# Gated delta rule in a 1-core fp32 network: the inverse of the 32x32 diagonal triangles by matmul levels, or by substitution on VectorE

## The chip, the cores and the metric

The kernel runs on one core of one Trainium2 chip. Its time is the device time of one launch in microseconds (us); of several runs the median counts. PE is TensorE, PEld its weight loads, DVE is VectorE, ACT is ScalarE, POOL is GpSimd, SP is the queue that issues the DMAs of this kernel. One row of the trace is one instruction; an f32 matmul shows as two rows, a matmul with fp32r operands as one.

## The reference, cut to what matters

The network is a mixer block with an MLP, then a gated delta-rule layer with 8 heads, a convolutional FFN, a sliding-window attention layer and a second FFN, on 512 positions of 1024 features. The change is in the delta-rule layer. With `q, k, v` of a head (512 x 128 each), `beta` and a decay `g` per position:

```python
decay = exp(where(i >= j, gc[i] - gc[j], -inf))      # gc: running sum of g inside a chunk
Lmat  = where(i > j, (k * beta) @ k.T * decay, 0)
sol   = triangular_solve(eye + Lmat, [v * beta, k * beta * exp(gc)])
# then, chunk by chunk:
v_new = value - k_cumdecay @ state
o     = q_dec @ state + attn_intra @ v_new
state = state * exp(gc_last) + k_dec.T @ v_new
```

The reference uses chunks of 64 positions; both kernels use 4 blocks of 128, which gives the same numbers in another grouping. Each head needs the inverse of four lower triangular 128x128 matrices with ones on the diagonal.

## The kernel before, in words

All activations are kept transposed (features on the 128 partitions, 512 positions along a row). A dense layer multiplies in three passes, hi*hi, hi*lo and lo*hi of a split into two fp32r parts (`mm3`, L269 to L273); a unit is one output tile of 128 features: 8 steps of `mm3`, 24 matmuls of 512 columns, into one of three PSUM buffers tagged `mm` (tile `m` in the trace). Five more PSUM buffers, tagged `aux` (tile `a`), serve all else. `weights` (L238) loads 512 KB by SP, rounds it on ACT (L247) and subtracts on DVE (L248); three buffers of each kind let it run three loads ahead.

The delta layer has 24 units for k, q, v of 8 heads, each followed by a causal convolution (`conv4`: L609, L610, three times L612, L614), and 8 gate units. `delta_begin` does the first 5 units, the scalars of all heads, and the decay matrices E of all 8 heads (`decay`: two matmuls L730 and L731 and four Exp on ACT, L734). `delta` then writes the rest out by hand with `weave`, which draws from several generators in proportion to the step counts given with them. While 23 steps of dense units are drawn, each of four stages moves on for one head each:

- `delta_a`: transposes of k, q, v, the norms (squares on ACT, L754 and L758, a Newton root on POOL), the matrix LT (L776), the matrix AT (L794), and kd, vb (L780, L781).
- `delta_b`: the inverse T of the four 32x32 diagonal triangles of each block by four levels, each of two rounds of four matmuls of 128x128 by 32 columns (`mmc`, L650), with masks on DVE (L807, L809), a DVE transpose (L643) and copies that spread the result on the diagonal (`expand`, L637, L639).
- `delta_b2`: merges 32 into 64 and 64 into 128 (L830, and `mm4` L657 on halves), then one correction step in f32 with two full rounds (L854, L860).
- `delta_c`: the recurrence over the four blocks (L875 to L899), the output norm (L903 to L911) and the transposes of the output.

Then `gated` (L974) multiplies by the gate and splits, and `OutProj` does the output layer; its first three tiles can start as heads become ready (`head`), the other five after all (`rest`). The order that each engine runs is not quite the order of the code: the framework takes the instructions by priority, which follows the code, but passes over those that it does not reckon ready, so a later dense matmul may stand before an earlier small one. At run time each engine keeps that fixed order.

Of the kernel before, what the change touches and what calls it, by code (L numbers as in the profile page):

```python
# [10 lines left out]
F32 = mybir.dt.float32  # L11
F32R = mybir.dt.float32r
# [53 lines left out]
SD = 6, 6, 13  # L66
FILL = 23
TAIL = (1.2, 1.3, 2.0, 3.0)
# [3 lines left out]
def _pack(i):  # L72
# [55 lines left out]
    for n in range(2):  # L128
# [14 lines left out]
    lev = [(((i[:, None] // (2 * s)) == (i[None, :] // (2 * s))) & ((i[:, None] // s) % 2 == 1)  # L143
            & ((i[None, :] // s) % 2 == 0)) for s in (1, 2, 4, 8, 16)]
    lev = [-t.astype(np.float32) for t in [lev[0].T] + lev[1:]] + [np.eye(P, dtype=np.float32)]
    a["levels"] = np.ascontiguousarray(np.concatenate(
        [np.concatenate([t[q:q + Q, q:q + Q] for q in range(0, P, Q)]) for t in lev], axis=1))
# [38 lines left out]
class Net:  # L186
    def __init__(self, ctx, tc, a, out, stages):
# [8 lines left out]
        self.sp = e(tc.tile_pool(name="sp", bufs=12))  # L196
        self.n = 0
# [435 lines left out]
    def expand(self, out, src):  # L633
        for i, q in enumerate(self.quads()):
            o, t = self.v4(out)[q, :, q], self.c4(src)[q]
            if i % 2:
                self.nc.scalar.copy(out=o, in_=t)  # L637
            else:
                self.nc.vector.tensor_copy(out=o, in_=t)  # L639

    def flip(self, src):
        t = self.sized(P, "cm", 6)
        self.nc.vector.transpose(out=t, in_=src.bitcast(F32))  # L643
        return t

    def mmc(self, lhs, rhs):
        ps = self.aux()
        for b in range(NB):
            c = slice(b * Q, (b + 1) * Q)
            self.nc.tensor.matmul(ps[:, c], lhsT=self.blk(lhs, b), rhs=rhs[:, c], start=True, stop=True)  # L650
        return self.c4(ps)

# [14 lines left out]
    def delta_scalars(self, ps, y):  # L667
# [47 lines left out]
        rows = self.hid(F32R)[0:ROWS]  # L715
        A.copy(out=rows, in_=pr[0:ROWS])
        lo = slice(Q, ROWS)
        V.tensor_tensor(out=rows[lo], in0=pr[lo], in1=rows[lo].bitcast(F32), op=ALU.subtract)
        sel = [self.hid(F32R)[0:ROWS] for _ in range(2)]
        for i, t in enumerate(sel):  # L720
            one = self.ident[0:ROWS, 4 * i:4 * i + 4].unsqueeze(2).to_broadcast([ROWS, 4, P])
            V.tensor_copy(out=self.v4(t), in_=one)
            V.tensor_copy(out=self.v4(t)[lo], in_=one[0:8])
# [23 lines left out]
    def delta_a(self, h):  # L747
        nc, d, s = self.nc, self.d, self.heads[h]
        V, A = nc.vector, nc.scalar
        E = self.E[h]  # L750
# [12 lines left out]
        sc = self.sized(20, "hs", 4)  # L763
        x, z, inv, rkl, rem = (sc[:, i * NB:(i + 1) * NB] for i in range(5))
        rk = r[:, 0:4]
        for o, t, u in ((x, rk, d["beta"][:, :, h]), (z, x, rk), (inv, v[:, 0:4], rk), (rkl, rk, d["ekl"][:, :, h]),
                        (rem, z, ss[:, 0:4])):
            nc.gpsimd.tensor_tensor(out=o, in0=t, in1=u, op=ALU.mult)
        nc.gpsimd.tensor_scalar(out=rem, in0=rem, scalar1=-1.0, scalar2=1.0, op0=ALU.mult, op1=ALU.add)
# [12 lines left out]
        yield  # L782
        LTr = self.hid(F32R)
        A.copy(out=LTr, in_=LT)
        LD, TD = (t[h % 2] for t in self.diag[:2])
        C, T = self.sized(P, "cm", 6), self.sized(P, "Tc", 3, F32R)
        for q in self.quads():
            A.copy(out=self.v4(LD)[q, :, q], in_=self.v4(LT)[q, :, q])
            V.tensor_tensor(out=self.c4(C)[q], in0=self.v4(LT)[q, :, q], in1=self.rep(self.lev[0], q), op=ALU.mult)
        V.tensor_tensor(out=self.c4(C), in0=self.c4(C), in1=self.rep(self.lev[5]), op=ALU.add)  # L790
# [6 lines left out]
        self.expand(TD, C)  # L797
        A.copy(out=T, in_=self.flip(C))
        self.heads[h] = dict(LT=LT, LTr=LTr, AT=AT, T=T, k=s["k"], kd=kd, vb=vb, q=s["q"], x=x, rem=rem, rq=r[:, 4:8])

    def delta_b(self, h):
        nc, d, s = self.nc, self.d, self.heads[h]
        V, A = nc.vector, nc.scalar
        T, (LD, TD, TL, TTL) = s["T"], (t[h % 2] for t in self.diag)
        for l in range(1, 5):
            M = self.sized(P, "cm", 6, F32R)
            V.tensor_tensor(out=self.c4(M), in0=self.mmc(LD, T), in1=self.rep(self.lev[l]), op=ALU.mult)  # L807
            yield
            V.tensor_tensor(out=self.c4(T), in0=self.mmc(TD, M), in1=self.c4(T).bitcast(F32), op=ALU.add)  # L809
            self.expand(TTL if l == 4 else TD, self.flip(T))  # L810
            yield
        self.expand(TL, T.bitcast(F32))

    def delta_b2(self, h):
        nc, d, s = self.nc, self.d, self.heads[h]
        V, A = nc.vector, nc.scalar
        LT, LTr = s["LT"], s["LTr"]
        T, TT = (t[h % 2] for t in self.diag[2:])
        T4, TT4, L4 = self.v4(T), self.v4(TT), self.v4(LTr)
        M = self.sized(P, "cm", 6, F32R)  # L820
        m4 = self.c4(M)
        pairs = [(slice(c, c + Q), slice(c + Q, c + 2 * Q)) for c in (0, 64)]

        def small(lo, hi, *fs):
            ps = self.aux()
            o = [self.c4(ps[:, i * P:]) for i in range(len(fs))]
            for t, f in zip(o, fs):
                for b in range(NB):
                    lhs, rhs = f(lo, hi, b)
                    nc.tensor.matmul(t[0:Q, b], lhsT=lhs, rhs=rhs, start=True, stop=True)  # L830
            return [t[0:Q] for t in o]

        for lo, hi in pairs:
            p, = small(lo, hi, lambda lo, hi, b: (L4[lo, b, hi], T4[lo, b, lo]))
            A.mul(m4[hi], p, -1.0)
        yield
        for lo, hi in pairs:
            p2, p3 = small(lo, hi, lambda lo, hi, b: (TT4[hi, b, hi], m4[hi, b]),
                           lambda lo, hi, b: (m4[hi, b], TT4[hi, b, hi]))
            A.copy(out=T4[hi, :, lo], in_=p2)  # L840
            V.tensor_copy(out=TT4[lo, :, hi], in_=p3)
        yield
        M = self.tmp(F32R)
        m4 = self.v4(M)
        top, bot = slice(0, 64), slice(64, P)
        p1 = self.mm4(LTr, T, k=top, m=bot, n=top)
        A.mul(m4[bot, :, top], self.v4(p1)[top, :, top], -1.0)
        yield
        p2, p3 = self.mm4(TT, M, k=bot, m=bot, n=top), self.mm4(M, TT, k=bot, m=top, n=bot)
        A.copy(out=T4[bot, :, top], in_=self.v4(p2)[top, :, top])  # L850
        V.tensor_copy(out=TT4[top, :, bot], in_=self.v4(p3)[top, :, bot])
        yield
        G = self.hid()
# [11 lines left out]
    def delta_c(self, h):  # L865
# [4 lines left out]
        for n in range(NB):  # L870
# [13 lines left out]
            if n < NB - 1:  # L884
                nc.tensor.matmul(p[:, 3 * P:], lhsT=B("kd"), rhs=vn, start=True, stop=True)  # L885
# [395 lines left out]
```

## Time and profile before

| | us |
|---|---|
| median of 3 runs | 1933.41 |
| the 3 runs | 1938.40, 1921.08, 1933.41 |
| span of the profiled execution, first to last instruction | 1936.9 |
| PE busy in it | 1901.8 (98%) |
| DVE busy | 1255.4 (65%) |
| ACT busy | 854.1 (44%) |
| mean granted clock of TensorE | 0.986 |

The span is that of one execution; the page gives no separate time for what lies around it, and the span lies inside the range of the three runs. The delta layer's decay block starts at 672.5 us of the span, its woven part ends about 977, and its last output tile about 1024. Busy time of PE counts overlapped rows once.

### The profile page before, as it was taken

To read this page: it belongs to the slowest core of one execution; us is meant where nothing else is said; L and a number is where in the kernel's file an instruction comes from. 1 tells how busy PE (TensorE), PEld (TensorE's weight loads), DVE (VectorE), ACT (ScalarE), POOL (GpSimd) and SP (SyncE) were. 2 spreads that over 40 slices of the span, in tenths; PEclk is the share of its full clock that TensorE was granted. 3 is DMA by queue.
4 is the path that set the end of the run, shared out by engine and by line. 5 is a ranking of instruction groups with operands and counts; after the bars stand their busy time and mean duration, and the time that the engine had idled before them with its cause. 6 is when DMAs were issued, how large, how long until landed. Compare 5 with 4: busy or idle time off the path is not lost.

```text
span 1936.9 us, 24978 instructions
## 1 busy us (share of the span) xinstructions
PE 1901.8 (98%) x9566; PEld 1587.6 (82%) x9566; DVE 1255.4 (65%) x2405; ACT 854.1 (44%) x1621; POOL 47.0 (2%) x162
## 2 busy tenths in 40 slices
PE   8999999999999999999999999999999999999997
PEld 6887888888889778888877888888889878888887
DVE  7999677324535847887776777743566567777434
ACT  5324443222333576675544444432367644444221
POOL 0010000000000011201000000000000000000000
PEclk9999999999999988998999999999999999999999
DMA  4222222222222211111122223222221122222221
GB/s 174 98 93 98 93 82 89 98 98 98 98 98 87 70 65 44 36 53 34 44 83 92 98 97 95 94 96 98 98 71 44 56 87 98 98 98 98 98 98 55
DMA packets 48520, 164.84 MB, mean 85 GB/s; under 512 B 5776, under 2 KB 8592, under 8 KB 48400
## 3 DMA queue, kind: packets, MB, share of 16 engines
q1 hardware_dynamic: 48400, 163.25, 24.4%
q8 instruction: 75, 1.23, 0.3%
q14 instruction: 45, 0.37, 0.1%
HBM read 161.13 MB, written 2.10 MB: 84 GB/s over the span
## 4 chain that ended last, share of the span: by engine, by line
PE 90%; DVE 5%; ACT 2%; issue 1%; POOL 0%; DMA 0%; SPq 0%; DVEq 0%; ACTq 0%
PE m L271 27%; PE m L272 27%; PE m L273 27%; PE a L657 1%; PE a L1207 1%; PE a L650 1%; PE a L623 1%; DVE t L612 1%; PE a L1146 1%; PE a L1188 1%; DVE wl L248 1%; ACT wh L247 1%; PE a L349 0%; PE a L880 0%; PE a L885 0%
## 5 line engine op out<-in xcount | busy, mean ns | idle before, releaser
L271 PE MATMUL m<-xh,wh 128*128 128x512 f32 (+1 forms) x1560 | 606.9, 392 | 10.9 <-ACT xh L305 7.0
L272 PE MATMUL m<-xl,wh 128*128 128x512 f32 (+1 forms) x1560 | 605.3, 389 | 0.5
L273 PE MATMUL m<-xh,wl 128*128 128x512 f32 (+1 forms) x1560 | 603.6, 388 | 0.5 <-DVE wl L248 0.5
L247 ACT CAST wh<-wr 128x1024 fp32r<-128x1024 f32 x302 | 316.6, 1051 | 604.3 <-PE m L272 473.4
L248 DVE TENSOR_TENSOR wl<-wr,wh 128x1024 fp32r<-128x1024 f32 x302 | 368.3, 1221 | 249.0 <-ACT wh L247 245.3
L271 PE MATMUL m<-h,wh 128*128 128x512 f32 (+1 forms) x984 | 362.7, 370 | 2.5 <-DVE x L1045 0.9
L273 PE MATMUL m<-h,wl 128*128 128x512 f32 (+1 forms) x984 | 362.9, 369 | 0.0
L272 PE MATMUL m<-h,wh 128*128 128x512 f32 (+1 forms) x984 | 362.8, 369 | 0.0
L271 PEld LDWEIGHTS m<-xh,wh 128*128 128x128 f32 x1560 | 294.2, 190 | 69.3 <-ACT xh L305 7.6
L273 PEld LDWEIGHTS m<-xh,wl 128*128 128x128 f32 x1560 | 296.0, 190 | 58.3 <-DVE wl L248 1.2
L272 PEld LDWEIGHTS m<-xl,wh 128*128 128x128 f32 x1560 | 295.8, 190 | 56.3 <-DVE xl L306 2.4
L271 PEld LDWEIGHTS m<-h,wh 128*128 128x128 f32 x984 | 185.3, 189 | 35.6 <-issue 2.0
L273 PEld LDWEIGHTS m<-h,wl 128*128 128x128 f32 x984 | 185.6, 189 | 31.7 <-DVE wl L248 0.9
L272 PEld LDWEIGHTS m<-h,wh 128*128 128x128 f32 x984 | 185.6, 189 | 31.5 <-issue 0.7
L1022 DVE SCALAR_TENSOR_TENSOR t<-t,vecs,t 128x511 f32<-128x511 f32 (+1 forms) x176 | 131.5, 747 | 4.9 <-ACT t L1020 1.8
L1019 DVE TENSOR_TENSOR t<-m,R 128x512 f32<-128x512 f32 x88 | 60.5, 687 | 83.3 <-PE m L273 83.3
L302 ACT CAST h<-t 128x512 fp32r<-128x512 f32 x80 | 49.6, 622 | 145.3 <-DVE t L1030 120.9
L497 DVE SCALAR_TENSOR_TENSOR h<-h,vecs,h 128x511 f32<-128x511 f32 (+28 forms) x120 | 82.3, 727 | 0.9 <-ACT h L494 0.9
L303 DVE TENSOR_TENSOR h<-t,h 128x512 fp32r<-128x512 f32 x80 | 55.1, 689 | 29.7 <-ACT h L302 29.5
L1020 ACT ACTIVATE t<-t,vecs 128x512 f32<-128x512 f32 x88 | 71.6, 814 | 1.7 <-DVE t L1019 1.6
L1028 ACT ACTIVATE t<-t 128x512 f32<-128x512 f32 x44 | 27.8, 632 | 85.2 <-DVE t L1022 85.2
L579 DVE TENSOR_TENSOR t<-m,R 128x512 f32<-128x512 f32 x32 | 22.1, 689 | 58.6 <-PE m L273 56.7
(268 smaller groups left out, 1688.6 us busy)
## 6 DMA issues: line engine op xcount, KB each, us to landing
wr<-in_f_up SPq DMA_DIRECT2D x88, 512.0 KB, 3.5
wr<-in_f_down SPq DMA_DIRECT2D x44, 512.0 KB, 3.4
wr<-in_w_up SPq DMA_DIRECT2D x32, 512.0 KB, 3.4
wr<-in_w_down SPq DMA_DIRECT2D x32, 512.0 KB, 3.4
wr<-in_a_w_in SPq DMA_DIRECT2D x32, 512.0 KB, 3.5
wr<-in_w_in SPq DMA_DIRECT2D x28, 512.0 KB, 3.5
wr<-in_w_o SPq DMA_DIRECT2D x8, 512.0 KB, 3.5
wr<-in_a_w_out SPq DMA_DIRECT2D x8, 512.0 KB, 3.5
```

Source lines behind the costliest of these rows:

```text
L247: nc.scalar.copy(out=wh, in_=raw)
L248: nc.vector.tensor_tensor(out=wl, in0=raw, in1=wh.bitcast(F32), op=ALU.subtract)
L271: nc.tensor.matmul(ps, lhsT=w[0], rhs=x[0], start=start, stop=False)
L272: nc.tensor.matmul(ps, lhsT=w[0], rhs=x[1], start=False, stop=False)
L273: nc.tensor.matmul(ps, lhsT=w[1], rhs=x[0], start=False, stop=stop)
L302: nc.scalar.copy(out=hi, in_=src)
L303: nc.vector.tensor_tensor(out=lo, in0=src, in1=hi.bitcast(F32), op=ALU.subtract)
L497: nc.vector.scalar_tensor_tensor(out=c[:, d:], in0=v[:, :S - d], scalar=wt[CONV_K - 1 - d], in1=c[:, d:], op0=ALU.mult, op1=ALU.add)
L1019: V.tensor_tensor(out=u, in0=ps, in1=R, op=ALU.mult)
L1020: A.activation(out=y, in_=u, func=AF.Identity, scale=w[2], bias=self.vec(f"f_b{i}", c))
L1022: V.scalar_tensor_tensor(out=y[:, d:], in0=u[:, :S - d], scalar=w[2 - d], in1=y[:, d:], op0=ALU.mult, op1=ALU.add)
L1028: A.activation(out=g, in_=g, func=AF.Silu)
```

## The change: what it does, and its diff

E is computed head by head inside `delta_a` instead of in `delta_begin`. LT gets the opposite sign. `delta_a` no longer makes the rounded copy and the compact copy of the diagonal; instead it writes the four 32x32 diagonal pieces of each block to a scratch in HBM (4 DMAs a head, runs of 128 bytes). `delta_solve` reads the 64 triangles of 4 heads back as 64 partitions of 1024 elements, does the forward substitution with 60 `tensor_tensor` on DVE, writes the inverse out and gathers it with one DMA as 128 partitions by 16 runs of 128 bytes. `delta_merge` merges 32 to 64 to 128 for 4 heads at once, in f32. The correction step is gone. `delta_c` writes `vn` over `vb` and the state over `kd`. The weave runs in two groups of 4 heads.

```diff
-SD = 6, 6, 13
-FILL = 23
-TAIL = (1.2, 1.3, 2.0, 3.0)
+SD = 6, 11, 14
+GROUP = 4
...
+        self.dp = e(tc.tile_pool(name="dp", bufs=4, space=bass.MemoryType.DRAM))
...
     def delta_a(self, h):
...
-        E = self.E[h]
+        E = self.decay(h)
...
+        nc.gpsimd.tensor_scalar(out=z, in0=z, scalar1=-1.0, scalar2=None, op0=ALU.mult)
...
+        L4, scr = self.v4(LT), self.scr[h // GROUP][0]
+        for i, q in enumerate(self.quads()):
+            nc.sync.dma_start(out=scr[h % GROUP, :, i].rearrange("b j i -> j b i"), in_=L4[q, :, q])
         kd, vb = self.hid(), self.hid()
...
-        LTr = self.hid(F32R)
-        A.copy(out=LTr, in_=LT)
...
-    def delta_b(self, h):
...
-    def delta_b2(self, h):
...
+    def delta_solve(self, g):
+        nc = self.nc
+        V = nc.vector
+        src, dst = self.scr[g]
+        W = self.sized(Q * Q, "solve", 1)[0:GROUP * 4 * NB]
+        nc.sync.dma_start(out=W, in_=src.rearrange("h b d j i -> (h b d) (j i)"))
+        S3 = W.rearrange("p (j i) -> p j i", i=Q)
+        n = GROUP * 4 * NB
+        yield
+        for j in range(1, Q - 1):
+            w = Q - 1 - j
+            t = self.sized(240, "outer", 2)[0:n, :j * w].rearrange("p (c i) -> p c i", i=w)
+            V.tensor_tensor(out=t, in0=S3[:, j:j + 1, j + 1:].to_broadcast([n, j, w]),
+                            in1=S3[:, 0:j, j:j + 1].to_broadcast([n, j, w]), op=ALU.mult)
+            V.tensor_tensor(out=S3[:, 0:j, j + 1:], in0=S3[:, 0:j, j + 1:], in1=t, op=ALU.add)
+            yield
+        V.memset(W[:, ::Q + 1], 1.0)
+        nc.sync.dma_start(out=dst.rearrange("h b d j i -> (h b d) (j i)"), in_=W)
+        TT = self.hid()
+        nc.sync.dma_start(out=TT.rearrange("p (h b i) -> p h b i", h=GROUP, b=NB),
+                          in_=dst.rearrange("h b d j i -> (d j) h b i"))
+        self.inv[g] = TT
+        yield
+
+    def delta_merge(self, g):
...
+        V.transpose(out=Tc, in_=TTc)
...
+        for k in (0, 2):
+            lo, hi = q[k], q[k + 1]
+            p = self.aux()
+            for i in range(n):
+                s, b = at(i)
+                T.matmul(p[0:Q, i * Q:(i + 1) * Q], lhsT=self.v4(s["LT"])[lo, b, hi], rhs=Tq[lo, i], start=True, stop=True)
+            (A.copy if k else V.tensor_copy)(out=M[hi], in_=p[0:Q])
             yield
+        for i, s in enumerate(hs):
+            for d in range(4):
+                o, t = s["t4"][q[d], :, q[d]], TTq[q[d], i * NB:(i + 1) * NB]
...
+        for i in range(n):
+            T.matmul(p[0:Q, i * Q:(i + 1) * Q], lhsT=TTq[q[1], i], rhs=Mq[q[1], i], start=True, stop=True)
+        A.copy(out=T64[q[1], :, 0:Q], in_=cq(p)[0:Q])
+        yield
+        for k in (0, 2):
+            p = self.aux()
+            for i in range(n):
+                T.matmul(p[0:Q, i * Q:(i + 1) * Q], lhsT=Mq[q[k + 1], i], rhs=TTq[q[k + 1], i], start=True, stop=True)
...
+        for h in range(0, GROUP, 2):
+            p, M = self.aux(), self.hid()
+            p4, M4 = (t.rearrange("p (n c) -> p n c", c=64) for t in (p, M))
+            for i in range(2 * NB):
+                s, b = at(h * NB + i)
+                T.matmul(p4[top, i], lhsT=self.v4(s["LT"])[top, b, bot], rhs=T64[top, h * NB + i], start=True, stop=True)
+            A.copy(out=M[bot], in_=p[top])
+            yield
+            p = self.aux()
...
+            for i in range(2 * NB):
+                s, b = at(h * NB + i)
+                T.matmul(p4[top, i], lhsT=M4[bot, i], rhs=s["t4"][bot, b, bot], start=True, stop=True)
...
-        self.E = [self.decay(h) for h in range(HEADS)]
...
     def delta(self):
...
-        for i in range(1, HEADS):
-            self.weave((islice(fill, FILL), FILL),
-                       *((f(i - 1 - j), n) for j, (f, n) in enumerate(stages) if i > j))
...
+        units = lambda n: (islice(fill, n * NT), n * NT)
+        a, c = self.delta_a, self.delta_c
+        self.weave(units(4), (chain(a(0), a(1)), 2 * SD[0]))
+        self.weave(units(3), (a(2), SD[0]))
+        self.weave(units(3), (a(3), SD[0]))
+        self.weave(units(6), (self.delta_solve(0), 36))
+        self.weave(units(1), (self.delta_merge(0), SD[1]))
+        self.weave(units(1), *((c(h), SD[2]) for h in range(4)))
+        self.weave(units(2), (chain(a(4), a(5)), 2 * SD[0]), (a(6), 2 * SD[0]))
+        self.weave(units(1), (a(7), SD[0]))
+        self.weave(units(5), (self.delta_solve(1), 36))
+        for h in range(4):
+            gated(h)
+        self.weave(units(1), (self.delta_merge(1), SD[1]))
 
         def rest():
             yield from fill
...
             yield from out.head(4)
...
+        self.weave((rest(), NT + 12), *((c(h), SD[2]) for h in range(4, 8)))
+        for h in range(4, 8):
+            gated(h)
         out.rest()
```

## Rows read from the trace of the kernel before

**Rows 1.** The page, part 1: busy time of each engine over the span
```profile
PE 1901.8 (98%) x9566; PEld 1587.6 (82%) x9566; DVE 1255.4 (65%) x2405; ACT 854.1 (44%) x1621; POOL 47.0 (2%) x162
```

**Rows 2.** Windows: us, then busy us (x instructions) per engine, clock, DMA
```profile
672.50:693.00 20.50, 20.27 (x43) 11.50 (x44) 5.29 (x8) 11.49 (x36) 0.00 (x0) 0.58 0.14 51
693.00:977.00 284.00, 275.79 (x1779) 233.69 (x1777) 220.19 (x698) 184.79 (x593) 37.40 (x144) 0.95 0.14 47
...
1030.00:1390.00 360.00, 359.08 (x1582) 296.47 (x1581) 223.52 (x279) 145.90 (x179) 0.00 (x0) 1.00 0.28 96
```

**Rows 3.** Timeline of PE in the decay block: start, us, instruction
```profile
673.13 0.50 PE L731 MATMUL a<-h,identr 128*128 128x512 f32 x1
673.57 0.50 PE L730 MATMUL a<-h,h 40*128 40x512 f32 x1
...
674.33 0.40 PE L271 MATMUL m<-xh,wh 128*128 128x512 f32 x1
```

**Rows 4.** Groups of PE by line in the delta layer (640 to 1030)
```profile
L731 PE MATMUL a<-h,identr 128*128 128x512 f32 x8 | 5.8, 720 | 0.0
```

**Rows 5.** Timeline of PE in the woven stretch, small matmuls in pieces
```profile
935.89 0.42 PE L657 MATMUL a<-t,h 64*64 64x64 f32 x4
936.14 0.40 PE L657 MATMUL a<-h,t 64*64 64x64 f32 x4
936.47 0.49 PE L880 MATMUL a<-h,h 128*128 128x128 f32 x2
936.71 0.47 PE L271 MATMUL m<-xh,wh 128*128 128x512 f32 x1
...
937.49 0.51 PE L650 MATMUL a<-Tc,h 128*128 128x32 f32 x4
937.85 0.66 PE L623 MATMUL a<-c,h 128*128 128x128 f32 x4
938.27 0.47 PE L271 MATMUL m<-xh,wh 128*128 128x512 f32 x1
...
939.49 1.06 PE L657 MATMUL a<-h,h 128*128 128x128 f32 x8
940.30 0.47 PE L271 MATMUL m<-xh,wh 128*128 128x512 f32 x1
...
944.38 0.31 PE L830 MATMUL a<-h,h 32*32 32x32 f32 x8
944.61 0.50 PE L271 MATMUL m<-xh,wh 128*128 128x512 f32 x1
```

**Rows 6.** Groups of DVE by line in the delta layer
```profile
L248 DVE TENSOR_TENSOR wl<-wr,wh 128x1024 fp32r<-128x1024 f32 x41 | 49.8, 1219 | 2.1 <-ACT wh L247 1.9
L612 DVE SCALAR_TENSOR_TENSOR t<-t,vecs,t 128x511 f32<-128x511 f32 (+2 forms) x57 | 41.9, 738 | 1.9 <-ACT t L610 1.5
...
L609 DVE TENSOR_TENSOR t<-m,R 128x512 f32<-128x512 f32 x19 | 13.0, 682 | 17.6 <-ACT h L614 15.5 <-PE m L273 2.0
...
L807 DVE TENSOR_TENSOR cm<-a,h 128x128 fp32r<-128x128 f32 x32 | 9.1, 286 | 8.7 <-PE a L650 8.4
```

**Rows 7.** Groups of ACT by line in the delta layer
```profile
L780 ACT ACTIVATE h<-a,hs 128x128 f32<-128x128 f32 x32 | 12.2, 382 | 0.4 <-POOL hs L768 0.3
...
L758 ACT ACTIVATE t<-a 128x128 f32<-128x128 f32 x32 | 8.5, 276 | 0.9 <-PE a L623 0.7
...
L758 ACT ACTIVATION_READ_ACCUMULATOR t<-a 128x1 f32 x32 | 6.6, 207 | 0.1
...
L614 ACT ACT_TABLE_LOAD x1 | 1.3, 1283 | 0.0
```

**Rows 8.** DMA queues, and issues with KB each and us to landing
```profile
q1 hardware_dynamic: 48400, 163.25, 24.4%
...
wr<-in_a_w_in SPq DMA_DIRECT2D x32, 512.0 KB, 3.5
```

**Rows 9.** Waits of the SP queue, 640 to 1000: us, times, longest
```profile
SPq L246 <- DVE wl L248: 231.1, 24, 27.5
```

More of the change, by code (lines that the diff above doesn't have):

```diff
@@ L631, in quads @@
             yield slice(q, q + Q)
[L633 to L651, printed above, removed]
     def mm4(self, lhs, rhs, k=slice(0, P), m=slice(0, P), n=slice(0, P)):
@@ L714, in delta_scalars @@
             nc.tensor.transpose(self.blk(pr, b)[0:ROWS], gx[:, b, :], self.ident)
-        rows = self.hid(F32R)[0:ROWS]
-        A.copy(out=rows, in_=pr[0:ROWS])
+        rows = self.hid(F32R)
+        nc.gpsimd.memset(rows.bitcast(F32), 0.0)
+        A.copy(out=rows[0:ROWS], in_=pr[0:ROWS])
         lo = slice(Q, ROWS)
         V.tensor_tensor(out=rows[lo], in0=pr[lo], in1=rows[lo].bitcast(F32), op=ALU.subtract)
-        sel = [self.hid(F32R)[0:ROWS] for _ in range(2)]
+        sel = [self.hid(F32R) for _ in range(2)]
         for i, t in enumerate(sel):
-            one = self.ident[0:ROWS, 4 * i:4 * i + 4].unsqueeze(2).to_broadcast([ROWS, 4, P])
+            one = self.ident[:, 4 * i:4 * i + 4].unsqueeze(2).to_broadcast([P, 4, P])
             V.tensor_copy(out=self.v4(t), in_=one)
@@ L781, in delta_a @@
             A.activation(out=self.blk(vb, b), in_=self.blk(pv, b), func=AF.Copy, scale=inv[:, b:b + 1])
-        yield
-        LTr = self.hid(F32R)
-        A.copy(out=LTr, in_=LT)
[L785 to L790, printed above, removed]
         yield
@@ L814, in delta_b2 @@
-    def delta_b2(self, h):
[L815 to L835, printed above, removed]
-        yield
[L837 to L853, printed above, removed]
-        p = self.mm4(LT, T.bitcast(F32))
-        for b in range(NB):
-            V.scalar_tensor_tensor(out=self.blk(G, b), in0=self.blk(T, b).bitcast(F32),
-                                   scalar=s["rem"][:, b:b + 1], in1=self.blk(p, b), op0=ALU.mult, op1=ALU.add)
-        yield
-        U = self.hid()
-        V.scalar_tensor_tensor(out=U, in0=TT.bitcast(F32), scalar=2.0, in1=self.mm4(G, TT.bitcast(F32)),
-                               op0=ALU.mult, op1=ALU.subtract)
-        yield
-        s["TT"] = U
@@ L880, in delta_c @@
             nc.tensor.matmul(p[:, 0:P], lhsT=B("TT"), rhs=w, start=True, stop=True)
-            vn = self.sized(P, "vn", 3)
-            A.activation(out=vn, in_=p[:, 0:P], func=AF.Copy, scale=s["x"][:, n:n + 1])
+            A.activation(out=w, in_=p[:, 0:P], func=AF.Copy, scale=s["x"][:, n:n + 1])
             yield
+            new = B("kd")
             if n < NB - 1:
-                nc.tensor.matmul(p[:, 3 * P:], lhsT=B("kd"), rhs=vn, start=True, stop=True)
-            nc.tensor.matmul(p[:, 2 * P:3 * P], lhsT=B("AT"), rhs=vn, start=True, stop=True)
+                nc.tensor.matmul(p[:, 3 * P:], lhsT=new, rhs=w, start=True, stop=True)
+            nc.tensor.matmul(p[:, 2 * P:3 * P], lhsT=B("AT"), rhs=w, start=True, stop=True)
             if n < NB - 1:
-                new = self.sized(P, "state", 3)
                 if n:
@@ L944, in delta_begin @@
         self.tri = self.const(a["tri"])
-        lv = self.hconst(a["levels"])
-        self.lev = [lv[:, i * Q:(i + 1) * Q] for i in range(6)]
         self.identr = self.cp.tile([P, P], F32R, name="identr")
@@ L953, in delta_begin @@
         self.delta_scalars(ps, y)
-        self.E = [self.decay(h) for h in range(HEADS)]
+        self.inv = [None] * (HEADS // GROUP)
+        self.scr = [[self.dp.tile([GROUP, NB, 4, Q, Q], F32, tag="scr", name=self.name("scr")) for _ in range(2)]
+                    for _ in range(HEADS // GROUP)]
         self.heads = [{} for _ in range(HEADS)]
@@ L965, in delta @@
         st, xs, R = self.begun
-        zero = self.hid()
-        nc.gpsimd.memset(zero, 0.0)
-        self.diag = [[self.hid(F32R) for _ in range(2)] for _ in range(4)]
-        for t in chain(*self.diag):
-            A.copy(out=t, in_=zero)
         self.gates = [None] * HEADS
```

71 lines of the change are left out of this document (34 added, 37 removed).

## Prediction

> **What bounds the kernel now.** I read the busy times first: PE is busy 98% of the span, DVE 65%, ACT 44%, POOL 47 us in all [rows 1]. A busy share doesn't say whether PE is near its peak, so the windows come next. In the first FFN, where nothing but dense matmuls runs, 1582 of them take 359.08 us, 0.227 us each [rows 2]; that is the price of a dense matmul at the full clock (2.4 GHz). The change acts on two other windows, the decay block (672.5 to 693) and the woven stretch (693 to 977). In the woven stretch PE is busy 275.8 of 284 us, DVE 220.2, ACT 184.8: PE is the bound, and DVE and ACT have 64 and 99 us of room. Of the clock, 0.05 of 284 us is lost there, 14 us, and in the decay block 0.42 of 20.5 us, 8.6 us, where PE runs partly at 1.2 GHz [rows 2]. So less PE work is worth its full time, as long as PE keeps finding other work. The timeline of the decay block shows how it finds some: a dense matmul (L271) of a unit that the code writes later stands between the decay matmuls [rows 3]. The order is by readiness, and dense units fill gaps while any are left.
>
> **The change part by part.** Prices of small matmuls are start to start, since busy times overlap [rows 5]: L650 four in 0.36 us, 0.090 each; L830 eight in 0.23, 0.029; the 64-wide L657 eight in 0.58, 0.073; the full f32 L657 eight records in 0.81, 0.101; two records of the recurrence 0.24; four transposes 0.42.
>
> Removed from PE, counted in the code: L650, 8 heads x 32 = 256 x 0.090 = 23.0; L830, 192 x 0.029 = 5.5; 64-wide merges, 96 x 0.073 = 7.0; the correction step, 64 f32 matmuls of two records, 128 x 0.101 = 12.9. Together 48.4 us.
>
> Added: the merge has 160 matmuls of 32x32 and 64 of 64x64. They are f32, so two records each: 320 x 0.029 + 128 x 0.073 = 18.6 us. The trace has no f32 matmul of 32x32; above, each record could cost a 128-row L650, 448 x 0.090 = 40 us; below, nothing is cheaper than 0.029. I take 18.6, the rows of the same shape.
>
> Moved: the 16 decay matmuls cost 0.72 us at the low clock [rows 4] and 0.44 at the full one (673.13 to 673.57, rows 3). Spread over the heads among dense matmuls they should not pull the clock down in one place. I take back the 8.6 us of lost clock; nothing if the fall only moves elsewhere. Net PE work: -48.4 + 18.6 - 8.6 = -38.4 us.
>
> What DVE gets. An operation of 128 columns takes 0.286 us and one of 512 takes 0.682 [rows 6], so 0.154 us plus 1.03 ns a column. The substitution has 30 steps of two operations of j(31-j) columns, 9920 in all: 60 x 0.154 + 10.2 = 19.5 us; if all 60 had the largest size, 240 columns, 24 us. I take 21, twice. DVE loses more than it gains over the stage (masks, transposes, copies, the correction), but its new work is lumped: in the first solve six units come with it, each 0.682 + 3 x 0.738 + 1.219 = 4.1 us of DVE [rows 6], 24.7 + 21 = 46 us against 144 x 0.227 = 32.7 us of PE. Three accumulators let PE run two units (11 us) ahead, so most of the 13 us is covered; what follows is store, gather and merge, with nothing for PE but later units. Without that cover 19 us, with it 0: E1 = 4.
>
> What ACT gets. Exp now stands in each head between the SiLUs of the units. The row shows one table load of 1.283 us where Exp gives way to SiLU [rows 7]; two per head are 2.6 us. With 8 squares of 0.276 + 0.207, 8 scalings of 0.382 and 4 Exp at that price, `delta_a` costs ACT 3.9 + 3.1 + 1.5 + 2.6 = 11 us and PE only 12 transposes x 0.105 + 16 x 0.101 + 2 x 0.44 = 3.8. Heads 4 to 7 come close together: 44 us of ACT. Beside them stand the recurrences of heads 0 to 3 and dense units, so E2 = 5, from 0 up to 25 if they don't.
> The Trainium skill, page "ScalarE: Activation LUTs", section "What ACT_TABLE_LOAD costs", gives about 1283 ns for the load and another 1380 ns of drain, 2.66 us a switch. By that the 16 switches would be an estimated 43 us of ACT instead of 21. The trace agrees on the first figure only; it has one instruction of 1.283 us and I count that.
>
> The new DMAs. Per head 4 stores wait on SP for LT; per group one load waits for 16 stores, one store for the solve, one gather for that store. Behind them in SP's queue wait the weight loads. SP already spends 231 us over 24 waits for a free buffer, up to 27.5 us each [rows 9], and loads run three ahead (3 x 5.45 us of PE), so a block of a few us costs nothing; one of over 16 us would stop PE. POOL's added memsets meet an engine nearly idle [rows 1]. A 512 KB weight load lands in 3.5 us [rows 8]; I take 3.5 for each leg and 5 for the gather of 2048 runs. Bounds: 3.5, and 20 us if each run cost what an average packet costs (24.4% of 16 x 1936.9 us over 48400 packets, 0.156 us; 2048 of them on 16 engines).
> The Trainium skill, page "DMA: Bandwidth & Descriptors", section "Specifications", wants 512 bytes or more per transfer for line rate; the 128-byte runs fall under that. No row here shows such runs.
>
> The tail is where the weave leaves PE alone. After LT of head 7 comes one chain: stores 3.5, load 3.5, solve 21, store 3.5, gather 5, DVE transpose 1, merge 15 (some ten dependent rounds of matmuls, 0.9 us, and a copy, 0.6), recurrence of four heads 20, their four norms one after another on DVE 14 (15 small operations at 0.16 and 4 at 0.28 a head), the gate product and split 2: 88 us. PE's own work in it: merge 9, recurrence 4 x (17 x 0.24 + 0.42) = 18, `out.head(4)` 36 x 0.227 = 8: 35 us. The 53 us left must be filled by gate units of 5.45 us, at most the last six (33 us); those that PE took earlier to fill a gap are missing. So 20 to 53 us idle; I take 26, five units left: E3 = 26. Before, the tail had 55 steps of dense work in reserve.
>
> The clock: idle PE and tiny matmuls in merges should bring stretches at 1.2 GHz that replace the 14 us lost before; E4 = +4, from -14 to +20.
>
> Sum: -38.4 + 4 + 5 + 26 + 4 = +0.6 us on a span of 1936.9. The median of the runs is 3.5 us under that span; I carry this over: **1934 us**. Removed PE time comes back as exposed chain.
>
> **The rivals.**
> *Chains hide (faster).* All six gate units are left for the second solve, and the four norms overlap the last blocks of the recurrence, so E3 is 10; E1, E2 and E4 are nil: -38 + 10 = -28, 1905 us. For it: PE's order is by readiness [rows 3], DVE and ACT have room [rows 2]. Against it: DVE and ACT work is lumped by phase.
> *The reserve is spent (slower).* Gate units are drawn into the gaps of the first group, PE sits idle 53 us in the tail, and starts merge and recurrence (27 us) and part of the output layer at 1.2 GHz, +16. With E1 and E2: -38 + 4 + 5 + 53 + 16 = +40, 1973 us. It decides where fewer than three gate units are left when the last solve starts (E3 over 37, with the clock). For it: the chain is serial by its data; the decay block shows that the clock falls in this stage [rows 2].
> *ACT sets the middle.* If heads 4 to 7 wait for ACT, E2 is 25: 1954 us. Against it: 99 us of room on ACT [rows 2].
> *The gather is slow.* At 20 us instead of 5, the tail grows by 15 and the first group by some 8: 1957 us. If the 128-byte runs are as costly as full packets it is this; the rule on 512 bytes above points the same way.
>
> **How the numbers follow.** About 1%, 19 us, is what a measurement of this kernel can tell from no change; the three runs alone differ by 17. Forecast, within 1%: 0.38, its own range 1915 to 1953. Chains hide: 0.34. Reserve spent: 0.18; ACT 0.05; gather 0.05: together 0.28 slower. The range reaches from 1893, into the faster case with cheaper merges, to 1970, just short of the full price of the spent reserve; the unknown matmul price (up to 21 us more) and the clock lie inside.
>
> **What would show it right or wrong.** L650 and L830 gone, about 450 records of 32 or 64 rows at 0.03 to 0.09 us; two runs of 60 DVE operations taking 20 to 24 us each; some 16 table loads; PE idle about 5 us around the first solve and 20 to 30 us from the last LT to the output layer; low clock there. It is wrong if PE stays over 97% busy through the second solve (faster), if idle PE time in the tail is over 40 us, or if a store or load of the scratch takes over 10 us to land.

## The result, and the profile after

The changed kernel takes 1945.78 us (median of 7 runs, 1945.28 to 1946.7), the kernel before 1933.41 beside it: ratio 1.0076, 95% interval 1.0052 to 1.01. By the 1% of the prediction that is no change, though the interval lies wholly on the slower side. The runs of before scatter over 17 us (1921.08 to 1938.4), those of the changed kernel over 1.4. The scatter goes with the clock: in 29 further executions of the kernel before the mean granted clock lies between 0.990 and 0.998, with 1934 to 1935 us at the one end and 1921 to 1922 at the other, and the profiled one, at 0.986, lost more than any of them. Variants of the changed kernel are therefore compared below with its own time, 1945.8 (1946.97 when run again), not only by ratios.

The head of the page of the changed kernel, and its clock by slice:

```profile
PE 1860.1 (96%) x9342; PEld 1559.8 (80%) x9342; DVE 1227.8 (63%) x2259; ACT 825.9 (42%) x1474; POOL 56.9 (3%) x164
...
PEclk9999999999999999789689999999999999999999
```

PE's busy time fell by 41.7 us against [rows 1], near the forecast 38.4, yet the span rose from 1936.9 to 1943.8: PE now has some 49 us more idle time, and the clock line has four slices under 9. The windows show where (columns: us, busy time of PE, PEld, DVE, ACT, POOL, then granted clock, DMA share, GB/s):

```profile
672.50:693.00 20.50, 17.77 (x94) 14.77 (x93) 13.00 (x25) 17.24 (x50) 6.25 (x17) 0.97 0.26 81
797.00:862.00 65.00, 50.90 (x435) 45.68 (x436) 30.18 (x141) 33.58 (x132) 3.33 (x10) 0.74 0.06 14
862.00:913.00 51.00, 43.82 (x231) 36.03 (x230) 32.48 (x81) 35.33 (x96) 14.88 (x64) 1.00 0.25 73
913.00:995.00 82.00, 52.58 (x419) 45.90 (x420) 47.28 (x181) 26.28 (x91) 2.38 (x5) 0.63 0.06 14
```

The first line answers to [rows 2]: the clock of the old decay block rose from 0.58 to 0.97. Idle PE time is 65 - 50.9 = 14.1 us from the gather of group 0 to the end of its norms, 7.2 while heads 4 to 7 are prepared, and 29.4 from the second solve to the output layer, with clocks of 0.74 and 0.63 in the two outer windows. No engine is full in any of them: a chain sets the time. PE's waits from 640 to 1040 name its links (us in all, times, longest):

```profile
PE m L267 <- DVE h L301: 16.5, 1, 16.5
PE a L618 <- DVE h L903: 15.5, 6, 3.6
PE a L818 <- DVE h L802: 9.6, 2, 6.6
PE a L618 <- DVE h L751: 6.4, 4, 2.7
```

The first wait is DVE's order: L301 splits the gated output of a first-group head for the output layer, and on DVE it stands behind the whole second solve. The second is the norms, the third the transpose that waits for the gather, the fourth LT. DVE's groups of the solve, both groups of heads together (names and shapes, count, busy, mean ns, idle before):

```profile
L780 DVE TENSOR_TENSOR outer<-solve 64x30 f32<-64x30 f32 (+14 forms) x60 | 19.3, 322 | 1.5
L782 DVE TENSOR_TENSOR solve<-solve,outer 64x30 f32<-64x30 f32 (+14 forms) x60 | 19.3, 321 | 1.3
L802 DVE STREAM_TRANSPOSE h<-h 128x512 f32<-128x512 f32 x2 | 1.4, 712 | 7.3 <-DMA h<-scr 7.3
```

That is 19.3 us a group (38.6 in all). SP's timeline gives the chain's dates (L755 stores of LT, L773 load, L785 store and L787 gather of the solved triangles; the first three lines are group 0):

```profile
744.13 0.61 SPq L773 DMA_DIRECT2D solve<-scr  x1
...
793.40 0.47 SPq L785 DMA_DIRECT2D scr<-solve  x1
797.65 0.39 SPq L787 DMA_DIRECT2D h<-scr  x1
...
895.07 1.73 SPq L755 DMA_DIRECT2D scr<-h  x4
898.10 0.47 SPq L773 DMA_DIRECT2D solve<-scr  x1
927.44 0.47 SPq L785 DMA_DIRECT2D scr<-solve  x1
930.43 0.39 SPq L787 DMA_DIRECT2D h<-scr  x1
```

From load to store the first solve takes 49.3 us, since DVE does other work between its steps, and the second 29.3. The DMA groups of the scratch (count, KB each, median us from issue to landing):

```profile
scr<-h SPq DMA_DIRECT2D x32, 16.0 KB, 1.5
solve<-scr SPq DMA_DIRECT2D x2, 256.0 KB, 4.5
scr<-solve SPq DMA_DIRECT2D x2, 256.0 KB, 3.6
h<-scr SPq DMA_DIRECT2D x2, 256.0 KB, 3.3
```

The gather of 2048 runs of 128 bytes lands in 3.3 us, faster than the load of as many bytes. Last, the timeline of PE in the second merge and in the norms of heads 4 to 7 (start, us, instruction, idle before it):

```profile
934.49 3.27 PE L818 MATMUL a<-h,h 32*32 32x32 f32 x61 [3.02 <-DVE h L802]
...
939.26 3.41 PE L836 MATMUL a<-h,h 32*32 32x32 f32 x64
942.60 1.97 PE L845 MATMUL a<-solve,h 64*64 64x64 f32 x16
...
979.74 1.12 PE L618 MATMUL a<-c,h 128*128 128x128 f32 x4 [3.59 <-DVE h L903]
...
991.81 1.65 PE L266 MATMUL m<-h,wh 128*128 128x512 f32 x3 [1.30 <-ACT h L300]
```

64 records of 32x32 take 3.34 us to the next group's start, 0.052 each; 16 of 64x64 take 1.89 to theirs (944.49), 0.118 each. From the last store of LT (895.07) to the output layer (991.81) it is 96.7 us; the prediction's chain had 88.

### The profile page after: what moved, and what is told of

It reads as the page before. It is cut to its first block, busy times and chain, and to the rows that moved or that the text cites. A ratio compares the mean times of both kernels' runs of the same rounds, so it can differ in the third digit from the quotient of the medians.

```text
span 1943.8 us, 24269 instructions
## 1 busy us (share of the span) xinstructions
PE 1860.1 (96%) x9342; PEld 1559.8 (80%) x9342; DVE 1227.8 (63%) x2259; ACT 825.9 (42%) x1474; POOL 56.9 (3%) x164
## 4 chain that ended last, share of the span: by engine, by line
PE 89%; DVE 5%; ACT 2%; POOL 2%; issue 1%; DMA 1%; DVEq 0%; SPq 0%; ACTq 0%; POOLq 0%
PE m L266 27%; PE m L267 27%; PE m L268 27%; PE a L1193 1%; PE a L1132 1%; PE a L618 1%; PE a L1174 1%; ACT wh L242 1%; DVE outer L780 1%; DVE solve L782 1%; POOL s L325 0%; PE a L873 0%; DVE wl L243 0%; PE a L344 0%; PE a L852 0%
## 5 line engine op out<-in xcount | busy, mean ns | idle before, releaser
L266 PE MATMUL m<-xh,wh 128*128 128x512 f32 (+1 forms) x1560 | 600.4, 388 | 10.4 <-ACT xh L300 6.3
L267 PE MATMUL m<-h,wh 128*128 128x512 f32 (+1 forms) x984 | 365.0, 371 | 16.5 <-DVE h L301 16.5
```

The costliest lines, as they stand in the source:

```text
L266: nc.tensor.matmul(ps, lhsT=w[0], rhs=x[0], start=start, stop=False)
L267: nc.tensor.matmul(ps, lhsT=w[0], rhs=x[1], start=False, stop=False)
```

## The experiments

**1 to 4: the tail's order, the solve, the clock, the decay.** The theory after reading the trace was that the two solve chains are exposed on PE; the rivals were DVE's order alone, the lost clock, and the moved decay.

`e1_gated_early` draws the gating of heads 0 to 3 before or inside the second solve:

```
-        self.weave(units(5), (self.delta_solve(1), 36))
-        for h in range(4):
+        for h in range(2):
             gated(h)
+        def early():
+            for h in (2, 3):
+                yield from islice(fill, NT)
+                gated(h)
+            yield from islice(fill, 3 * NT)
+        self.weave((early(), 5 * NT), (self.delta_solve(1), 36))
```

> The changed kernel with the gate products of heads 0 to 3 drawn before and inside the second solve instead of behind it. In the changed kernel the output layer's second matmul waits 16.5 us for L301 on VectorE, which stands behind the solve. Theory 'order' (the exposed chain costs what it does because work that could fill it is queued behind the solve on VectorE): the 36 matmuls of the output layer's head run inside the solve, the wait on L301 goes, and what they took inside merge and recurrence (about 36 x 0.23 to 0.43 us) goes from the path: 1932 to 1938 us, against 1945.8. Rival 'chain' (the chain is serial, what runs beside it is free): within 2 us of 1945.8. Rival 'clock': the filled wait also keeps TensorE at 2.4 GHz into the merge, another 8 us less: 1925 to 1932.

Measured: 1943.58 us, ratio 1.0065 (1.0046 to 1.0084), 2.2 us under the changed kernel: the rival 'chain', at the edge of its 2 us. The wait on L301 is gone, and in PE's list of waits another has grown in its place:

```profile
PE a L818 <- DVE h L802: 20.5, 2, 14.2
```

PE runs the output layer's first part earlier and then waits for the same gather. A wait of 16.5 us was worth 2 us: it stood beside the chain, not on it.

`e2_no_subst` leaves 29 of the 30 substitution steps out (`for j in range(1, 2)`):

> The changed kernel with 1 of the 30 substitution steps left in each group (the other 29 are left out, so the inverse of the 32x32 triangles is not computed). Theory 'chain': the second solve stands wholly on the path, 24.8 us of it, the first one is covered by dense units; the time falls by 20 to 26 us, to 1920 to 1926. Rival 'covered': VectorE's work is hidden in both groups and PE finds other work: a fall of under 6 us. Rival 'both exposed': the first solve costs too, a fall of over 35 us.

Measured: 1904.92 us, ratio 0.986 (0.9836 to 0.9884). 41 us less than the changed kernel, for some 38 us of DVE work taken out: the rival 'both exposed' held. Its second load on SP's timeline, and the dense matmuls alone (tile `m`) between the first load and the first store, here and in the changed kernel (columns as above, without POOL):

```profile
881.49 0.47 SPq L773 DMA_DIRECT2D solve<-scr  x1
```

```profile
745.90:751.80 5.90, 5.90 (x28) 4.89 (x27) 0.69 (x1) 0.00 (x0) 1.00 0.51 144
```

```profile
744.00:793.40 49.40, 49.40 (x220) 40.90 (x219) 4.75 (x7) 0.00 (x0) 1.00 0.30 101
```

The load comes 16.6 us earlier than the 898.10 of the changed kernel; the other 23.0 us of the 39.6 between the spans (1943.8 and 1904.2) stand behind it. PE doesn't idle beside the first solve, yet that solve costs its 16.6 us: the cover is 220 dense matmuls, 9.2 units where the code draws six, and the units taken ahead are missing in later gaps. From 755 to 820 PE idles 0.2 us here; in the changed kernel, in as long a stretch behind its solve (797 to 862), 14.1. DVE is busy for 63% of the span and still sets the time here.

`e3_warm` puts 18 unused 512-column matmuls beside the second solve:

```
+        def warm():
+            p, t = self.aux(), self.heads[7]["AT"]
+            for _ in range(18):
+                nc.tensor.matmul(p, lhsT=t[:, 0:P], rhs=t, start=True, stop=True)
+                yield
-        self.weave(units(5), (self.delta_solve(1), 36))
+        self.weave((chain(islice(fill, 5 * NT), warm()), 5 * NT + 18), (self.delta_solve(1), 36))
```

> The changed kernel with 18 further f32 matmuls of 512 columns (about 0.9 us each, 16 us in all, results unused) after the third-to-last gate tiles, in the wait for the second solve. Theory 'clock': the merge and the first half of the recurrence of heads 4 to 7 then run at 2.4 instead of 1.2 GHz and the time falls by 6 to 12 us, although PE has more to do. Rival 'chain': the merge is paced by its dependent rounds, the clock does little: within 2 us of 1945.8. Rival 'PE': the added work lands on the path, slower by up to 16 us.

Measured: 1942.66 us, ratio 1.0062 (1.0043 to 1.0081), 3 us less. The windows before and in its second merge (columns as in the first windows):

```profile
930.00:936.30 6.30, 5.78 (x13) 4.18 (x13) 4.30 (x11) 1.46 (x3) 2.37 (x5) 0.50 0.64 138
936.30:940.50 4.20, 4.20 (x124) 4.14 (x124) 1.15 (x4) 3.28 (x10) 0.00 (x0) 0.91 0.02 4
940.50:946.00 5.50, 5.50 (x61) 4.78 (x59) 1.12 (x4) 1.49 (x5) 0.00 (x0) 0.50 0.00 0
```

The merge begins near the full clock and falls to 1.2 GHz at about 940 with PE busy throughout. Its first 64 records take 2.04 us to the next group's start, 0.032 each, against 0.052 at the low clock. So the price of a 32x32 record at full clock was nearly right (0.029), and a warmer start buys little: from the merge's first matmul to the recurrence's it is 17.1 us, in the changed kernel 19.1. Not all of the 3 us are the clock's: the solve itself is 1.5 us shorter here (27.9 from load to store), since the spare matmuls push a unit's DVE work behind it.

`e4_decay_moved` is the kernel before with one line of the change: `E = self.decay(h)` in `delta_a`, and the eight calls in `delta_begin` dropped.

> The kernel before with one part of the change alone: E computed per head at the start of delta_a instead of for all heads in delta_begin. The prediction took 8.6 us of lost clock back for this: about 1925 us. Rival 'the fall of the clock only moves': within 4 us of 1933. Rival 'ACT': 16 more table loads of 1.283 us at the start of each head's stage hold ACT up, slower by 5 to 15 us.

Measured: 1917.46 us, ratio 0.9934 (0.9914 to 0.9954): faster than both kernels. The same two windows as [rows 2], of this kernel:

```profile
672.50:693.00 20.50, 19.73 (x100) 16.62 (x101) 14.63 (x26) 19.86 (x47) 4.46 (x18) 1.00 0.20 74
693.00:977.00 284.00, 276.54 (x1809) 229.71 (x1809) 225.32 (x722) 204.82 (x621) 33.14 (x126) 1.00 0.14 48
```

The clock is at its full level in both; of before's windows the first had 0.58 and the second 0.95. One part of the change is thus a gain of some 14 us (1931.2 to 1917.5), and all the rest together costs about 28. Most of the 14 is clock that is not lost: beside the executions of before that were granted 0.998 too (1921 to 1922 us), the gain is 4 to 5.

**5 to 8: the tail's stagger, the price of the old inverse, the decay undone, the gather.**

`e5_stagger` changes the weave's step counts and gates each head behind its own recurrence:

```
+        lead = (2.0, 1.6, 1.25, 1.0)
-        self.weave(units(1), *((c(h), SD[2]) for h in range(4)))
+        self.weave(units(1), *((c(h), SD[2] * lead[h]) for h in range(4)))
...
+        def cg(h):
+            yield from c(h)
+            gated(h)
...
-        self.weave((rest(), NT + 12), *((c(h), SD[2]) for h in range(4, 8)))
+        self.weave((rest(), NT + 12), *((cg(h), SD[2] * lead[h - 4]) for h in range(4, 8)))
```

> The changed kernel with another order only: in both groups the heads' merge and recurrence get different step counts in the weave (2.0, 1.6, 1.25 and 1.0 times as many), so that they no longer run in step, and the gate unit of a head is drawn right after that head's recurrence instead of after all four. If the idle 29 us of the tail come from four heads waiting at the same place of their chains at once (merge together, recurrence together, then norms with nothing for PE), staggering lets the norm of one head stand beside the recurrence of another: PE idle between the last solve and the output layer falls by 8 to 14 us, 1932 to 1938 us. If the chain of one head behind the solve sets the end, whatever the order, the time stays within 4 us of the changed kernel's 1945.8, or rises where the head that comes last gets later.

Measured: 1944.96 us, ratio 1.0087 (1.007 to 1.0104), no gain by the time, as in the second case of the expectation. But on SP's timeline its second load of the solve stands later:

```profile
904.87 0.47 SPq L773 DMA_DIRECT2D solve<-scr  x1
```

That is 6.8 us behind 898.10, and the span is 1943.2: behind the load it is 1038.3 us, against 1045.7 in the changed kernel. The stagger shortened the tail by some 7 us and delayed the first group by as much. Staggering the second group alone was not tried.

`e6_no_inverse` is the fourth kernel with the level loop's four rounds and the correction step left out:

> The kernel before with the decay matmuls moved into delta_a (the earlier run e4_decay_moved, 1917.5 us) and with the old triangular inverse cut: the four rounds of the level loop (two sets of block matmuls each) and the correction step are left out, so that the triangle's inverse is not formed. It prices the work that the change replaces, without what it puts there. By the prediction's prices L650 is 23.0 us of PE and the correction 12.9, together about 36: if PE sets the time throughout, 1917.5 - 36 = about 1881 us. If the level loop ran mostly beside other PE work, in gaps where PE waited for DVE anyway, the gain is under 20 us: 1898 to 1915. If the old chain was exposed too (PE waited for it), the gain is over 45 us: under 1872.

Measured: 1890.2 us, ratio 0.9801 (0.9783 to 0.9819), so 0.0133 under the fourth kernel's ratio, 26 us. The page's first part for the fourth kernel and for this one:

```profile
PE 1882.4 (98%) x9566; PEld 1573.1 (82%) x9566; DVE 1254.8 (65%) x2405; ACT 872.4 (46%) x1637; POOL 47.2 (2%) x162
```

```profile
PE 1846.0 (98%) x9182; PEld 1534.0 (81%) x9182; DVE 1216.1 (64%) x2237; ACT 856.1 (45%) x1589; POOL 51.6 (3%) x162
```

36.4 us of PE work went, where the prediction's prices gave 23.0 + 12.9 = 35.9. The time fell by 10 us less, between the expected cases: part of the old inverse ran where PE had nothing else, and PE's idle time rose from 33.6 us to 42.0 without it. So some 26 us were to be had by replacing these parts with something free, and the exposed solves alone cost 41.

`e7_E_begin` is the changed kernel with the eight calls of `decay` back in `delta_begin`:

> The changed kernel with one part undone: the decay matmuls and their Exp of all eight heads go back into delta_begin, as in the kernel before; all else stays changed. If the parts add up, the move that was worth 14 us in the kernel before (1931.2 to 1917.5) is lost here: 1958 to 1962 us, with a stretch at 1.2 GHz near 675 us as before. If the changed kernel's clock falls for other reasons anyway (idle PE in the merges), the move is worth only its 8.6 us of the decay block or less: 1948 to 1955. If ACT's 16 switches between Exp and the other functions had a cost in the middle of the stage, the time falls: 1935 to 1943.

Measured: 1937.61 us, ratio 1.0046 (1.0025 to 1.0067), 8 us less than the changed kernel. The move that gains 14 us in the kernel before loses 8 in the changed one; the third case of the expectation held, and no stretch at 1.2 GHz came back near 675. Its second load on SP's timeline, and then its first window:

```profile
891.00 0.47 SPq L773 DMA_DIRECT2D solve<-scr  x1
```

```profile
672.50:693.00 20.50, 19.43 (x100) 15.59 (x99) 9.71 (x14) 17.92 (x63) 4.72 (x14) 1.00 0.23 78
```

The load comes 7.1 us earlier, and the span is 8.0 shorter. The clock of the window is 1.00, with the decay block in it (before: 0.58), so here the move had no lost clock to win back; the last section returns to this. ACT's timeline of the changed kernel shows what stood in front of it, up to the squares of head 7:

```profile
874.97 1.28 ACT L609 ACT_TABLE_LOAD   x1
876.26 0.63 ACT L609 ACTIVATE h<-t 128x512 f32<-128x512 f32 x1
876.90 1.28 ACT L710 ACT_TABLE_LOAD   x1
878.19 1.14 ACT L710 ACTIVATE h<-a,d 128x128 f32<-128x128 f32 x4
...
881.58 1.28 ACT L917 ACT_TABLE_LOAD   x1
882.87 0.63 ACT L917 ACTIVATE h<-t 128x512 f32<-128x512 f32 x1
883.52 1.28 ACT L710 ACT_TABLE_LOAD   x1
884.82 1.14 ACT L710 ACTIVATE h<-a,d 128x128 f32<-128x128 f32 x4
885.83 0.29 ACT L730 ACTIVATE t<-a 128x128 f32<-128x128 f32 x1
```

From 874.97 to 885.83 ACT has no pause: four table loads (5.1 us), two sets of Exp (2.3), the SiLUs of dense units and the scalings of another head. Head 7's squares wait for all of it, and its LT, the load and the solve wait for head 7. The fourth kernel has 16 more table loads too and gains all the same: PE is busy there for 276.5 of the 284 us of the woven stretch, so no wait for a late head shows.

The Trainium skill, page "ScalarE: Activation LUTs", section "What ACT_TABLE_LOAD costs", adds some 1380 ns of drain to a load of 1283 at every switch. The trace disagrees on the drain: the load at 874.97 takes 1.28 and the SiLU starts at 876.26.

`e8_no_gather` replaces store and gather by two DVE copies, without the rearrangement, which is left out:

```
-        nc.sync.dma_start(out=dst.rearrange("h b d j i -> (h b d) (j i)"), in_=W)
-        nc.sync.dma_start(out=TT.rearrange("p (h b i) -> p h b i", h=GROUP, b=NB),
-                          in_=dst.rearrange("h b d j i -> (d j) h b i"))
+        for i in range(2):
+            V.tensor_copy(out=TT[64 * i:64 * i + 64], in_=W[:, S * i:S * i + S])
```

> The changed kernel with the store of the solved triangles and the gather behind it (two DMAs per group, 4.5 and 3.3 us) taken out: two DVE copies put the solved tile into the tile that the gather filled, without its rearrangement, which is left out. It prices the round trip behind the solves. If the chain solve, store, gather, merge is exposed in both groups, each group gains about 6 to 8 us: 1930 to 1934 us. If the first group's trip is hidden by dense units and only the second is exposed: 1937 to 1940. If PE merely waits at the next place: within 4 us of 1945.8.

Measured: 1940.77 us, ratio 1.0066 (1.0048 to 1.0083), 5 us less. Its second load on SP's timeline:

```profile
897.70 0.46 SPq L773 DMA_DIRECT2D solve<-scr  x1
```

So of the first group's trip 0.4 us were left by that date (1.9 against 899.60, its date when the changed kernel was run again), and the rest of the gain lies behind it, near the middle case. PE's wait for the first gather, the 6.6 us above, is 1.1 us here; that so little of it reaches the second load means that something in between takes it up, and what does was not settled.

**9 to 12: what else could stand beside the second solve.**

`e9_two_beside` moves two recurrences of the first group:

```
-        self.weave(units(1), *((c(h), SD[2]) for h in range(4)))
+        self.weave(units(1), *((c(h), SD[2]) for h in range(2)))
...
-        self.weave(units(5), (self.delta_solve(1), 36))
+        self.weave(units(5), (self.delta_solve(1), 36), *((c(h), SD[2]) for h in range(2, 4)))
```

> The changed kernel with one move: the recurrences of heads 2 and 3 are taken out of the first group's weave and drawn beside the second solve; all the work is there. If PE idles in the second solve for want of work, these two recurrences (about 9 us of PE work by the prediction's count) fill part of the 16.5 us wait behind L301, and the heads of the second group start earlier: 1931 to 1938 us. If the recurrence of two heads is as long as that of four (a chain, not work), nothing is gained in the first group, and the solve, interleaved on DVE with the recurrences' own operations, gets longer: 1944 to 1952. Beside it stands the changed kernel, run again in the same call.

Measured: 1942.05 us, ratio 1.0083 (1.0065 to 1.01), 4.9 us under the changed kernel run again beside it (1946.97): between the two cases. Only its times are used here.

`e10_begin_beside` is this edit on the seventh kernel:

> The two edits together: decay and Exp of all heads in delta_begin (1937.6 us alone) and the recurrences of heads 2 and 3 beside the second solve. If both are gains on different waits they add: 1924 to 1930 us. If the second edit is worth nothing, 1936 to 1940.

Measured: 1931.75 us, ratio 1.0027 (1.0013 to 1.0041). From 1937.6 that is 5.9 less, so the two edits add, though the time stays 1.8 us above the expected 1924 to 1930. SP's timeline shows both sides of the edit:

```profile
876.96 0.47 SPq L773 DMA_DIRECT2D solve<-scr  x1
912.19 0.47 SPq L785 DMA_DIRECT2D scr<-solve  x1
```

The load comes 14 us earlier than in the seventh kernel, but from load to store it is now 35.2 us instead of 29.4: the recurrences' DVE operations stand between the steps of the solve.

`e11_E_together` draws the decay and Exp of heads 4 to 7 in one place, behind the first solve:

```
-        E = self.decay(h)
+        E = self.decay(h) if h < GROUP else self.E[h - GROUP]
...
         self.weave(units(6), (self.delta_solve(0), 36))
+        self.E = [self.decay(h) for h in range(GROUP, HEADS)]
```

> The changed kernel with the decay matmuls and Exps of heads 4 to 7 drawn together, right behind the first solve and before the first merge, where PE and ACT wait for the gather; heads 0 to 3 as in the changed kernel. If the table switches between Exp and SiLU in front of the second solve are what the run with all eight in delta_begin gained, the same gain is here: the last heads' store moves some 6 us forward, 1936 to 1941 us. If that gain came from the first heads or from the clock in the decay block, nothing here: 1943 to 1948.

Measured: 1935.16 us, ratio 1.0042 (1.0024 to 1.0061), 11.8 under the changed kernel run again beside it; more than expected. The second load on SP's timeline of this kernel, and of the changed kernel run again:

```profile
888.52 0.47 SPq L773 DMA_DIRECT2D solve<-scr  x1
```

```profile
899.60 0.47 SPq L773 DMA_DIRECT2D solve<-scr  x1
```

> The changed kernel, unaltered, for a comparison on one chip with the three runs beside it: 1943 to 1948 us by its earlier runs. A version that is under it by more than 3 us here is faster than it.

Measured: 1946.97 us, ratio 1.0109 (1.0094 to 1.0124). Of the 12.1 us between their spans (1945.4 and 1933.3) 11.1 stand in the date of this load. It is about what ACT no longer does on the way there: in the repeat one table load and two sets of Exp ahead of head 4 (3.6 us from 855.17 on), and four loads and two sets behind it, as shown above (7.4). From the load to the end of the span it is 1045.7 us in the changed kernel, 1045.8 in its repeat, 1044.8 in the seventh and 1044.8 in the eleventh. What these two move ahead of the second load is won in full; that is what a critical chain looks like. Where an edit changes the solve or what follows, the date alone doesn't tell the gain: 1041.2 in the eighth run, 1049.9 in the tenth.

## Why the prediction was right

The forecast, 1934 us and within 1%, held: the time is within 1% of before, 12 us above the forecast. 5.5 us of these are the step "the median of the runs is 3.5 us under that span": it was carried over, but the changed kernel's runs lie 1.5 to 3 us over its span (1945.3 to 1946.7 against 1943.8). Before's median lay under the span because the profiled execution had lost more clock than most. The other 6.3 are in the span (1943.8 against 1936.9 + 0.6). The mechanism, removed PE work that comes back as exposed chain, is what the runs show; that the terms sum to so little error is in part luck, as they miss in both directions:

- **PE work removed and added.** 41.7 us of busy time went, 38.4 were forecast, and two errors cancel in that. The old inverse was priced right (36.4 for 35.9 of it, sixth run). The merge was not: 18.6 us was its price at full clock, and it ran at 1.2 GHz, 320 x 0.052 + 128 x 0.118 = 32 us; the bound of 40 was the nearer end. The moved decay gave more than its 8.6: the fourth kernel's PE is busy 19.4 us less than before [rows 1] with no matmul gone. With these, -48.4 + 32 - 19.4 = -35.8; some 6 us stay open, of which the padding (last section) is worth some 2.
- **Decay block.** The 8.6 us came back (0.58 to 0.97 in that window). In the kernel before the move is worth 14 by the medians, since the later lost clock of [rows 2] (0.05 of 284 us) goes with it; it depends on how much clock an execution loses.
- **Solve.** 19.3 us a group for 21. Both are exposed (second run), where the sum had the first covered but for E1 = 4.
- **E1, around the first solve: 4.** Beside the first solve PE idles little (4.5 us from 695 to 797), as forecast; behind it, up to the end of group 0's norms, 14 us. The sum counted the cover of the solve, not gather, merge and norms of the first group, and it took the cover as free, though it was paid with units that these and the tail then lacked (second run: the first solve costs 16.6 us). This is the mis-sized term.
- **E2, ACT in the middle: 5.** PE's idle time there is 7.2 us, near the forecast; but the seventh and eleventh runs win 8 and 12 us by taking Exp out, because the delay moves the second load and with it the whole tail. The rival "ACT sets the middle" (25 us, 1954) had the right mechanism at less than half its price.
- **E3, the tail: 26.** From the last store of LT to the output layer PE idles 32.9 us, the row below (29.4 from 913 on), a little over the 20 to 30 that were named as a sign. The chain is 96.7 us, not 88, and the reserve was smaller than the five units taken: after the load at 898.1 dense units last until 909, about two. That is the condition of the rival "the reserve is spent", whose 53 us did not follow: PE's own work in the tail, at the low clock, filled more of the chain (49.9 us from 909 on, for 35 in the sum).

```profile
895.07:991.81 96.74, 63.80 (x475) 54.74 (x473) 61.27 (x216) 36.15 (x107) 2.38 (x5) 0.70 0.13 37
```

- **E4, the clock: 4.** More is lost than before (0.74 and 0.63 in two windows), but beside a chain it seems to cost little: the second merge is 2 us shorter when it begins warm (third run). What the low clock costs in all was not measured.
- **The rivals.** "Chains hide" asked for 1905; 1904.9 is what the kernel takes with nearly no substitution at all. "The gather is slow" falls with 3.3 us. The Trainium skill, page "DMA: Bandwidth & Descriptors", section "Specifications", asks for 512 bytes or more a transfer for line rate. The trace shows no price at this size: the gather's 128-byte runs land in 3.3 us, the load of as many bytes in 4.5.

So removed PE time did come back as exposed chain, term by term larger in the first group than forecast. The pairing of a gain with a loss was not seen: the decay move is a gain in the kernel before, where the clock falls in the decay block, and a loss in the changed one, where it doesn't and a chain hangs on ACT.

## What to carry to other kernels

Once a serial chain sets the end, busy shares and even the largest wait of the bound engine mislead: a wait of 16.5 us was worth 2, while the date of one load on SP's queue told the gains of 8 and 12 us to about a microsecond. Price an edit by asking whether it moves the last input of that chain; small work on an engine that is half idle (two Exps and four table loads) counts in full when it stands in front of that input. And try the parts of a change alone: one line of this one makes the kernel before faster (1917.5 us), mainly by its clock, and the rest hides it.

## What was not expected of the hardware

A PE that is busy all the time can run at the low clock. In the kernel before, from 675.2 to 692.3 us (columns as above):

```profile
675.20:692.30 17.10, 17.10 (x33) 9.52 (x33) 2.10 (x3) 9.26 (x29) 0.00 (x0) 0.50 0.17 61
```

17.1 of 17.1 us busy at 1.2 GHz, with the decay matmuls (L730 of 40 rows, L731) among dense ones. The change also pads L730's operands from 40 to 128 rows with zeros, which the prediction counted only as POOL's memsets. In the seventh kernel the same block, padded, stays at the full clock (1.00 in the window shown there). Padding also makes the two decay matmuls of a head cheaper at that clock: 0.46 us from the start of the first to the start of the next instruction in the changed kernel (from 671.69), 0.76 in the fourth, with 40 rows (from 720.15).

And in the third run the clock fell inside a gapless series of 32x32 matmuls. What makes the difference stays open: before's block also follows 1.02 us of idle PE, padding alone was not tried, and the executions of before don't all lose as much (0.986 to 0.998 with the same matmuls).
